# Memory gates moved to the seven-product jobs, branch sums added on VectorE, two squares of the residual put off

## Chip, core and metric

One Trainium2 chip, one of its NeuronCores. The metric is the time of one launch on the device, in microseconds; three runs of the kernel before gave a median of 1319.66 us (1317.09 to 1323.9). The core has five engines with queues of their own (TensorE = PE, VectorE = DVE, ScalarE = ACT, GpSimd = POOL, SyncE = SP) and 16 DMA engines that all queues share. SP computes nothing here; it issues nearly all transfers, in the order of its queue.

## The reference

One layer of a streaming encoder for 640 tokens (512 of a prompt, 8 x 16 of samples), width 1024, all in float32. The part that matters:

```python
xn = rmsnorm(x, norm_mix_g)
u, v, cq, ckv, kr, qm, ga, gb, gc = split(xn @ w_in)        # one combined projection
o_gm, o_mla, o_mem = gMLP(u, v), latent_attention(cq, ckv, kr), memory_attention(qm)
merged = (sigmoid(ga) * (o_gm @ w_br_gm)
          + sigmoid(gb) * (o_mla @ w_br_mla)
          + sigmoid(gc) * (o_mem @ w_br_mem))
h = x + merged @ w_out
y = h + (silu(hn @ ffn_w_gate) * (hn @ ffn_w_up)) @ ffn_w_down   # hn = rmsnorm(h, norm_ffn_g)
```

The sigmoid is made as (tanh(g/2) + 1), with the factor 1/2 in the weights.

## The kernel before

**Two ways to multiply.** Every float32 operand is split into a high and a low part, and one product is three matmuls (low weight x high data, high x high, high x low). `lin` does a block of 128 outputs plainly: 8 slices of the inner dimension, two halves of 320 tokens, three matmuls, so 48 matmuls of 128x320, with a weight of 128x1024 that ACT casts (L84) and DVE subtracts (L79). The later stage, `post`, uses a scheme of seven products for two by two blocks: a job makes 256 outputs by seven products of 12 matmuls, 84 matmuls where the plain way takes 96. Its weights come as four quarters of 128x512 (`wraws`, L1064), and sums of quarters are made on DVE (`wq`, L1048 and L1054). Sums of the data blocks (tiles `xc`) are made once and serve every job on the same data.

**Order of the stages.** Memory keys and attention; the memory branch (about 185 to 330 us), in which the latent attention's first projections and the samples' queries are interleaved; latent attention; then `post`: jobs in pairs, the two jobs' products alternating, for u and the gates of gMLP and latent attention; then the branch products of latent attention (`mla`, four jobs) and gMLP (`gm`, four jobs), each by eight direct products "a" to "h", 96 matmuls; then the output projection (`w_o`, four jobs), gate/up and down.

**The memory branch.** `branch` goes through 8 blocks of 128 outputs. A block is a gate (48 matmuls `psb<-xh` or `xl`) and a product with `w_br_mem` (48 matmuls `psb<-oh` or `ol`); `merge` scales the gate on DVE, takes the tanh on ACT, and multiplies on DVE into the accumulator `acc`, which is stored to `accspill` every two blocks. From block 3 on the samples' queries lie in between (`cqs`, `qns` and `tmp,perm` in the rows). Raw weights go through one pool of `WR` slots, three here.

**The branch sums.** A `mla` job loads its stored gate (tile `th`), multiplies it with the products (L1380) and stores the result to `tdram` (`t<-th`). In the first `gm` pair `acc_load` loads the four parts of `accspill` into `raw`, and four transfers on POOL's queue add the `t` parts to it in flight (L1447):

```python
raw_load(sa, [self.accd[j] for j in range(4)])()
for j in range(4):
    nc.gpsimd.dma_start(out=sa["t"][:, j], in_=tdram[j], accum_op=ALU.add)
```

The `gm` jobs then add their own products to `raw` (L1383), and from `raw` DVE and ACT make the data blocks of the output projection. Tiles `th` and the loads of h share a pool of five slots.

**The residual.** `out_job` adds a job's products to a part of x, stores it, squares it on ACT (L1478) and adds the square into `rbc` on DVE (L1483). `stats` makes the norm of it before the last product of the first gate/up job.

Of the kernel before, what the change touches and what calls it, by code (L numbers as in the profile page):

```python
# [18 lines left out]
T = 640  # L19
# [37 lines left out]
class Builder:  # L57
# [153 lines left out]
    def build(self):  # L211
        tc, nc, a = self.tc, self.nc, self.a
        ctx = ExitStack()
        pool = lambda name, side="left", **kw: tc.alloc_tile_pool(name=name, bufs=1, side=side, reuse_waits="tile", **kw)
        self.pool = pool
        self.WB, self.WR = 2, 3
        self.wx, self.wn = None, 0
        cp = pool("const")
        self.ap = pool("acc")
        self.tp = pool("tmps")  # L220
        self.wp = pool("wts", "right")
        self.pp = None
        self.psum(sc=6, tr=1, pv=1)

        self.ident = cp.tile([128, 128], F32, name="ident")
        self.ones = cp.tile([128, 128], F32, name="ones")
        self.gvec = cp.tile([128, 45], F32, name="gvec")
        self.mhalf = cp.tile([128, 8], F32, name="mhalf")
        self.rbc = cp.tile([128, T], F32, name="rbc")
        nc.gpsimd.memset(self.ones, 1.0)  # L230
        nc.gpsimd.memset(self.mhalf, -0.5)
        self.dma(self.gvec, a["gvec"])
        self.rtok = cp.tile([128, 8], F32, name="rtok")
        nc.scalar.activation(self.rtok, self.mhalf, AF.Exp)
# [12 lines left out]
        self.mem_branch(s2, ob)  # L247
        ob.release()
        x1.release()

        self.mla(s2)
        s2.release()
        self.post()
        self.tp.release()
        self.ap.release()
        cp.release()
        self.pp.release()
# [297 lines left out]
            out.append((h, l))  # L555
        return out

    def merge(self, m, pg, z, first):

        nc = self.nc  # L560
        th = self.tmp()
        self.scaled(th, pg)
        nc.scalar.activation(th, th, AF.Tanh, scale=0.5)
        if first:
            if m == 0:
                self.accT = self.ap.tile([128, 8, T], F32, tag="acc", bufs=1, name="acc")
            self.acc[m] = self.accT[:, m, :]
            nc.vector.scalar_tensor_tensor(self.halves(self.acc[m]), self.halves(th), 1.0, z, op0=ALU.add, op1=ALU.mult)
        else:
            nc.vector.scalar_tensor_tensor(self.halves(th), self.halves(th), 1.0, z, op0=ALU.add, op1=ALU.mult)  # L570
            nc.gpsimd.tensor_tensor(self.acc[m], self.acc[m], th, op=ALU.add)

    def gate(self, n, m):
        w = self.wload(self.a["w_g_" + n][m], 1024)
        pg = self.psb()
        self.lin(pg, w, self.xs)
        return pg

    def branch(self, n, os_, first=False, hooks={}, pg=None):
        a = self.a  # L580
        if first:
            self.acc = [None] * 8
        for m in range(8):
            if m or pg is None:
                pg = self.gate(n, m)
            for f in hooks.get(2 * m, ()):
                f()
            w = self.wload(a["w_br_" + n][m], 1024)
            po = self.psb()
            self.lin(po, w, os_)  # L590
            self.merge(m, pg, po[:, :, :HN], first)
            if m % 2:
                self.dma(self.accd[m // 2], self.accT[:, m - 1:m + 1, :])
            for f in hooks.get(2 * m + 1, ()):
                f()

# [57 lines left out]
    def mem_branch(self, s2, ob):  # L654

        a = self.a
        tp = self.pool("s2t")
        self.mla_consts(s2)
        st = {}

        def ckv():
            st["ckv"] = self.proj(tp, [0, 1])
            st["kr"] = self.proj(tp, [2])[0]

        def rckv():
            st["rkv"] = self.squared(st["ckv"])

        def nckv():
            self.ckvn, self.ckvs = self.normed(st["ckv"], st["rkv"], G_KV, "ckv")
            for k in range(2):  # L670
                self.dma(a["ckvT_o"][128 * k:128 * k + 128, :], st["ckv"][k])

        def cq():
            self.rope_key(st["kr"])
            st["cq"] = self.proj(tp, [3, 4, 5])

        def rcq():
            st["rq"] = self.squared(st["cq"])

        def ncq():  # L680
            self.cqn, self.cqs = self.normed(st["cq"], st["rq"], G_Q, "cq")

        ckv()
        os_ = self.split_o(self.omem, ob)
        hooks = HOOKS(rckv, nckv, cq, rcq, ncq)
        for pr in range(4):
            hooks[7 + 2 * pr] = [lambda pr=pr: self.sample_qn(s2, pr)]
            hooks[8 + 2 * pr] = [lambda pr=pr: self.sample_qr(pr)]
        self.branch("mem", os_, first=True, hooks=hooks)
        tp.release()  # L690
        self.t2.release()

# [516 lines left out]
    def post(self):  # L1209
# [69 lines left out]
        for tag, bufs in (("r21", 3), ("r22", 3), ("ws", 2), ("wl", HB), ("wh", HB), ("r12", 2), ("r11", 2)):  # L1279
            self.W.tile([128, 512], F32R if tag[0] == "w" and tag != "ws" else F32, tag=tag, bufs=bufs, name=tag)  # L1280

        gdram = {n: [self.tc.dram_tile([128, 2, T], F32, name="g" + n + str(j)) for j in range(4)] for n in ("mla", "gm")}

        def gate_job(n, j):
            cnt = []

            def done(g, q):
                cnt.append(q)
                if len(cnt) == 4:
                    nc.scalar.activation(g, g, AF.Tanh, scale=0.5)  # L1290
                    self.dma(gdram[n][j], g)
            return {"ap": a["w_g_" + n][j], "kp": 4, "xc": xc, "ev": self.ev_form(lambda: pair("g"), done)}

        def u_job(j):
            cnt = []
# [57 lines left out]
        jobs[0][1]["post"] = {2: [v_end(0)], 3: [v_end(1)]}  # L1353
        jobs += [[u_job(j), gate_job("gm", j)] for j in range(4)]
        jobs[1][0]["post"] = {2: [v_end(2)]}
        jobs += [[gate_job("mla", 2), gate_job("mla", 3)]]
        for x in jobs[2:]:
            x[1]["post"] = {5: [run_later], 2: [run_later]}
        pairs = [(x, self.LATER) for x in jobs]
# [5 lines left out]
        xb, make = self.operands(src, True)  # L1365


        tdram = [self.tc.dram_tile([128, 2, T], F32, name=f"t{j}") for j in range(4)]

        def branch_job(n, j, xb):  # L1370
            st = {}

            def load():
                st["th"] = pair("th")
                self.dma(st["th"], gdram[n][j])

            def ev(q, ps):
                ix = (slice(None), q[0], slice(HN * q[1], HN * q[1] + HN))
                t = st["th"][ix]
                nc.vector.scalar_tensor_tensor(t, t, 1.0, ps, op0=ALU.add, op1=ALU.mult)  # L1380
                if n == "gm":
                    acc = sa["t"][:, j][ix]
                    nc.vector.tensor_tensor(acc, acc, t, op=ALU.add)  # L1383
                elif q == (1, 0):
                    self.dma(tdram[j], st["th"])
            return {"ap": a["w_br_" + n][j], "kp": 4, "xc": xb, "ev": ev, "load": load}

        def raw_load(src, tiles):
            def f():
# [50 lines left out]
        add_d([branch_job("gm", j, xb) for j in range(4)])  # L1440
        sa = {}
        xo, mko = self.operands(sa)

        def acc_load():
            raw_load(sa, [self.accd[j] for j in range(4)])()
            for j in range(4):
                nc.gpsimd.dma_start(out=sa["t"][:, j], in_=tdram[j], accum_op=ALU.add)  # L1447
        hook(pairs[-2][0][0], "a", acc_load, "pre")
        B = pairs[-1][0][1]
        for at, f in (("a", lambda: (mko(1, 0, 2), mko(5, 0, 2))), ("b", lambda: (mko(6, 0, 2), mko(3, 0, 2))), ("c", lambda: mko(7, 0, 2)),  # L1450
                      ("d", lambda: (mko(1, 2, 4), mko(5, 2, 4))),
# [5 lines left out]
        sh = {}  # L1457
        xf, make = self.operands(sh)
        s = self.rbc

        def out_job(j):
            st = {}
# [8 lines left out]
            def done(q):  # L1471
# [3 lines left out]
                nc.scalar.activation(sh["t"][:, j, m, ns], h[:, m, ns], AF.Copy, scale=self.g(G_FFN + 2 * j + m))  # L1475
                if q == (1, 0):
                    self.dma(self.hdram[j], h)
                    nc.scalar.activation(h, h, AF.Square)  # L1478
                    if j == 0:
                        nc.vector.tensor_tensor(s, h[:, 0, :], h[:, 1, :], op=ALU.add)  # L1480
                    else:
                        for m in range(2):
                            nc.vector.tensor_tensor(s, s, h[:, m, :], op=ALU.add)  # L1483
            return {"ap": a["w_o"][j], "kp": 4, "xc": xo, "ev": lambda p, ps: st["ev"](p, ps), "load": load}

        out = [out_job(j) for j in range(4)]
# [33 lines left out]

        n0 = len(pairs)
        add([x for j in range(NF // 2) for x in gu_jobs(j)])
        hook(pairs[n0][0][0], 7, stats, "pre")

        ys = {}

# [136 lines left out]
def _prepare(i):  # L1663
# [20 lines left out]
    for p in range(128):  # L1684
# [13 lines left out]
        "w_qm": _pack(wqm),  # L1698
        "ck": mk.reshape(8, 256, 4, 2, 128).transpose(2, 0, 4, 3, 1),
        "cv": mv.reshape(8, 2, 128, 4, 256).transpose(3, 0, 2, 1, 4),  # L1700
        "w_g_gm": _packs(ga), "w_g_mla": _packs(gb), "w_g_mem": _pack(gc),
        "w_br_gm": _packs(i["w_br_gm"][0]), "w_br_mla": _packs(i["w_br_mla"][0]), "w_br_mem": _pack(i["w_br_mem"][0]),
        "w_kvq": _pack(np.concatenate([wckv, wkr, wkr, wcq], 1)),
        "w_uqn": uqn,
# [42 lines left out]
```

## Time and profile before

| | |
|---|---|
| median of three runs | 1319.66 us |
| profiled execution | 1319.9 us, of which span 1318.2 us |
| PE busy | 1272.3 us (97%), 8800 matmuls |
| DVE busy | 954.7 us (72%) |
| ACT busy | 640.5 us (49%) |
| POOL busy | 67.4 us (5%) |
| mean granted clock of TensorE | 0.995 of full speed |

The span runs from the first to the last instruction; 1.7 us of the execution lie around it. PE's matmuls are pipelined, so that the duration of one says little; the distance from start to start is what a matmul costs. A few per cent of the matmul records are missing from the trace.

### The profile page before, as it was taken

The numbers are of one execution on the slowest core, as the hardware profiler recorded it, in microseconds if no ns is written. First come the engines' busy times: TensorE is split into PE (matmuls) and PEld (weight loads), VectorE is DVE, ScalarE is ACT, GpSimd is POOL, SyncE is SP. The second block draws the span as 40 slices with busy tenths as digits, with TensorE's granted clock in tenths as the row PEclk, the third lists the DMA queues.
The fourth block names the chain that finished last, engine by engine and source line by source line (L and its number), as shares of the span: only waits on it lengthen the run. The fifth ranks groups of instructions, "written<-read, shape, count | busy, mean of one in ns | idle before, by whom it ended". The sixth has DMA issues, their size and how long they took to land.

```text
span 1318.2 us, 22764 instructions
## 1 busy us (share of the span) xinstructions
PE 1272.3 (97%) x8800; PEld 1226.9 (93%) x8800; DVE 954.7 (72%) x1723; ACT 640.5 (49%) x1263; POOL 67.4 (5%) x84
## 2 busy tenths in 40 slices
PE   7899999999999999999999999989999999998997
PEld 7898899999988889899999999989999999998997
DVE  7844354432578787688874457998889888899986
ACT  6734342222466656585554222665455455655444
POOL 5200001000000120000000000000000000000000
PEclk9999999999999999999999999999999999999999
DMA  7874622233532462243368862426344334342443
GB/s 228 261 265 160 211 95 90 76 113 120 171 90 80 160 234 81 73 144 133 134 227 294 258 197 88 133 80 195 119 135 137 103 101 136 101 164 86 145 133 122
DMA packets 83020, 193.56 MB, mean 147 GB/s; under 512 B 8480, under 2 KB 21920, under 8 KB 82912
## 3 DMA queue, kind: packets, MB, share of 16 engines
q1 hardware_dynamic: 80416, 182.93, 41.6%
q0 software_dynamic: 2224, 8.91, 2.5%
q8 instruction: 69, 1.13, 0.4%
q14 instruction: 39, 0.32, 0.1%
q10 hardware_dynamic: 272, 0.26, 0.1%
HBM read 159.41 MB, written 31.62 MB: 145 GB/s over the span
## 4 chain that ended last, share of the span: by engine, by line
PE 62%; DVE 18%; DMA 8%; issue 7%; ACT 4%; POOL 0%; SPq 0%; POOLq 0%; DVEq 0%; ACTq 0%
PE psb L65 18%; PE psX L1111 15%; PE psc L65 11%; PE psY L1111 6%; DVE wl L79 6%; PE psv L65 4%; PE psZ L1111 3%; DVE xc L79 2%; DVE ws L1054 2%; PE ppv L65 1%; DMA wr<-in_w_fd 1%; DMA wr<-in_w_fu 1%; ACT wh L84 1%; PE ptr L65 1%; DMA wr<-in_w_o 1%
## 5 line engine op out<-in xcount | busy, mean ns | idle before, releaser
L84 ACT CAST wh<-wr 128x512 fp32r<-128x512 f32 (+5 forms) x372 | 219.5, 610 | 216.7 <-PE psX L1111 62.4
L79 DVE TENSOR_TENSOR wl<-wr,wh 128x512 fp32r<-128x512 f32 (+5 forms) x372 | 253.1, 694 | 77.9 <-ACT wh L84 77.5
L1111 PE MATMUL psX<-xc,wh 128*128 128x320 f32 x1344 | 298.1, 310 | 0.0
L1111 PEld LDWEIGHTS psX<-xc,wh 128*128 128x128 f32 x1344 | 226.1, 189 | 0.0
L1111 PE MATMUL psX<-xc,wl 128*128 128x320 f32 x672 | 210.4, 313 | 12.3 <-DVE th L1380 4.9
L1111 PE MATMUL psY<-xc,wh 128*128 128x320 f32 x672 | 150.2, 310 | 0.0
L1111 PEld LDWEIGHTS psX<-xc,wl 128*128 128x128 f32 x672 | 126.8, 189 | 17.5 <-DVE th L1380 5.7
L84 ACT CAST wh<-ws 128x512 fp32r<-128x512 f32 x138 | 85.0, 619 | 77.2 <-DVE ws L1054 64.0
L1111 PEld LDWEIGHTS psY<-xc,wh 128*128 128x128 f32 x672 | 113.5, 189 | 0.0
L1111 PE MATMUL psY<-xc,wl 128*128 128x320 f32 x336 | 105.2, 313 | 7.6 <-DVE wl L79 5.7
L79 DVE TENSOR_TENSOR wl<-ws,wh 128x512 fp32r<-128x512 f32 x138 | 93.1, 685 | 17.9 <-ACT wh L84 17.2
L1111 PE MATMUL psZ<-xc,wh 128*128 128x320 f32 x400 | 89.2, 311 | 0.0
L65 PE MATMUL psb<-xh,wl 128*128 128x320 f32 x352 | 83.1, 317 | 0.0
L65 PE MATMUL psb<-xl,wh 128*128 128x320 f32 x352 | 80.9, 310 | 0.0
L65 PE MATMUL psb<-xh,wh 128*128 128x320 f32 x352 | 80.2, 309 | 0.0
L1111 PEld LDWEIGHTS psY<-xc,wl 128*128 128x128 f32 x336 | 63.6, 189 | 10.0 <-DVE wl L79 7.8
L1111 PEld LDWEIGHTS psZ<-xc,wh 128*128 128x128 f32 x400 | 67.3, 189 | 0.5 <-issue 0.5
L65 PEld LDWEIGHTS psb<-xh,wl 128*128 128x128 f32 x352 | 57.5, 188 | 5.9 <-issue 5.8
L1111 PE MATMUL psZ<-xc,wl 128*128 128x320 f32 x200 | 62.2, 311 | 0.0
L1054 DVE TENSOR_TENSOR ws<-ws,wr 128x512 f32<-128x512 f32 x92 | 61.5, 683 | 0.1
L84 ACT CAST xc<-raw 128x1280 fp32r<-128x1280 f32 (+1 forms) x36 | 37.3, 1054 | 47.8 <-DVE raw L1383 19.0
L65 PEld LDWEIGHTS psb<-xh,wh 128*128 128x128 f32 x352 | 58.8, 188 | 0.0
(406 smaller groups left out, 2927.6 us busy)
## 6 DMA issues: line engine op xcount, KB each, us to landing
wr<-in_w_fg SPq DMA_DIRECT2D x44, 256.0 KB, 3.4
wr<-in_w_fu SPq DMA_DIRECT2D x44, 256.0 KB, 3.7
cache<-in_ck SPq DMA_DIRECT2D x8, 1024.0 KB, 8.2
cache<-in_cv SPq DMA_DIRECT2D x8, 1024.0 KB, 7.4
wr<-in_w_fd SPq DMA_DIRECT2D x32, 256.0 KB, 3.7
aspill<-g SPq DMA_DIRECT2D x11, 640.0 KB, 3.1
raw<-aspill SPq DMA_DIRECT2D x11, 640.0 KB, 5.3
wr<-in_w_ft SPq DMA_DIRECT2D x32, 192.0 KB, 2.5
```

The costliest lines, as they stand in the source:

```text
L65: i = self.nc.tensor.matmul(out, lhsT=l, rhs=r, start=start, stop=stop)
L79: self.nc.vector.tensor_tensor(out, a, b, op=ALU.subtract)
L84: self.nc.scalar.copy(h, src)
L1054: nc.vector.tensor_tensor(src, x, z, op=ALU.add)
L1111: self.nc.tensor.matmul(ps, lhsT=lw[:, ws], rhs=rx[:, k, :], start=first and k == 0 and i == 0, stop=last and k == kp - 1 and i == 2, skip ...
```

## The change

- The memory gates leave `branch`. They become four seven-product jobs in two pairs behind the last pair of latent-attention gates. `branch` keeps only the products with `w_br_mem`; ACT copies them into a tile `z`, stored to `accspill`. A memory gate job loads its part of `z`, takes the tanh and forms (tanh + 1) x z with one DVE instruction of 128x1280; the result is stored to `gmem`.
- A `mla` job loads its part of `gmem` beside its gate, adds it to its own product on DVE (128x1280, L1373 after) and stores the sum over `accspill`. The `gm` pair loads `accspill` alone: the `tdram` tiles and the four adding transfers of POOL are gone.
- The squares of output jobs 2 and 3 are made after products 6 and 3 of the second job of the first gate/up pair, and `stats` after its product 7.
- The raw-weight pool has four slots, and `w_g_mem` is packed in quarters.

```diff
-        self.WB, self.WR = 2, 3
+        self.WB, self.WR = 2, 4
...
-    def branch(self, n, os_, first=False, hooks={}, pg=None):
+    def branch(self, os_, hooks):
+
         a = self.a
-        if first:
-            self.acc = [None] * 8
+        z = self.ap.tile([128, 8, T], F32, tag="acc", bufs=1, name="z")
         for m in range(8):
-            if m or pg is None:
-                pg = self.gate(n, m)
             for f in hooks.get(2 * m, ()):
                 f()
-            w = self.wload(a["w_br_" + n][m], 1024)
+            w = self.wload(a["w_br_mem"][m], 1024)
             po = self.psb()
             self.lin(po, w, os_)
-            self.merge(m, pg, po[:, :, :HN], first)
+            self.nc.scalar.copy(self.halves(z[:, m, :]), po[:, :, :HN])
             if m % 2:
-                self.dma(self.accd[m // 2], self.accT[:, m - 1:m + 1, :])
+                self.dma(self.accd[m // 2], z[:, m - 1:m + 1, :])
...
         def gate_job(n, j):
             cnt = []
+            st = {}
+
+            def load():
+                st["z"] = pair("z")
+                self.dma(st["z"], self.accd[j])
 
             def done(g, q):
                 cnt.append(q)
                 if len(cnt) == 4:
                     nc.scalar.activation(g, g, AF.Tanh, scale=0.5)
+                    if n == "mem":
+                        nc.vector.scalar_tensor_tensor(g, g, 1.0, st["z"], op0=ALU.add, op1=ALU.mult)
                     self.dma(gdram[n][j], g)
-            return {"ap": a["w_g_" + n][j], "kp": 4, "xc": xc, "ev": self.ev_form(lambda: pair("g"), done)}
+            return {"ap": a["w_g_" + n][j], "kp": 4, "xc": xc, "ev": self.ev_form(lambda: pair("g"), done),
+                    "pre": {6: [load]} if n == "mem" else {}}
...
-        jobs += [[gate_job("mla", 2), gate_job("mla", 3)]]
+        jobs += [[gate_job("mla", 2), gate_job("mla", 3)]] + [[gate_job("mem", j), gate_job("mem", j + 1)] for j in (0, 2)]
...
+            def more():
+                st["z"] = pair("z")
+                self.dma(st["z"], gdram["mem"][j])
...
                 elif q == (1, 0):
-                    self.dma(tdram[j], st["th"])
-            return {"ap": a["w_br_" + n][j], "kp": 4, "xc": xb, "ev": ev, "load": load}
+                    nc.vector.tensor_tensor(st["th"], st["th"], st["z"], op=ALU.add)
+                    self.dma(self.accd[j], st["th"])
+            return {"ap": a["w_br_" + n][j], "kp": 4, "xc": xb, "ev": ev, "load": load, "pre": {"d": [more]} if n == "mla" else {}}
...
-        def acc_load():
-            raw_load(sa, [self.accd[j] for j in range(4)])()
-            for j in range(4):
-                nc.gpsimd.dma_start(out=sa["t"][:, j], in_=tdram[j], accum_op=ALU.add)
-        hook(pairs[-2][0][0], "a", acc_load, "pre")
+        hook(pairs[-2][0][0], "a", raw_load(sa, [self.accd[j] for j in range(4)]), "pre")
...
                 if q == (1, 0):
                     self.dma(self.hdram[j], h)
-                    nc.scalar.activation(h, h, AF.Square)
-                    if j == 0:
-                        nc.vector.tensor_tensor(s, h[:, 0, :], h[:, 1, :], op=ALU.add)
+                    if j < 2:
+                        squares()
                     else:
-                        for m in range(2):
-                            nc.vector.tensor_tensor(s, s, h[:, m, :], op=ALU.add)
+                        late.append(squares)
...
-        hook(pairs[n0][0][0], 7, stats, "pre")
+        for p in (6, 3):
+            hook(pairs[n0][0][1], p, lambda: late.pop(0)())
+        hook(pairs[n0][0][1], 7, stats)
```

PE's queue in the memory branch, where the queries of one pair of heads for the samples begin, before (`cqs` and `qns` are the samples' latent and query, `xh` and `xl` the gate's data, `wr` a raw weight):

```order
L65 MATMUL psb<-cqs,wr 128x128 x6
L65 MATMUL psb<-xh,wl 128x320 x2
L65 MATMUL psb<-xh,wh 128x320 x2
L65 MATMUL psc<-qns,wr 128x128 x4
L65 MATMUL psb<-xl,wh 128x320 x2
L65 MATMUL psb<-xh,wl 128x320 x2
...
L65 MATMUL psb<-xl,wh 128x320 x2
L65 MATMUL psc<-cqs,wr 128x128 x3
L65 MATMUL psb<-oh,wl 128x320 x2
L65 MATMUL psb<-oh,wh 128x320
L65 MATMUL psc<-tmp,perm 128x128
```

and the same place after:

```order
L65 MATMUL psb<-cqs,wr 128x128 x6
L65 MATMUL psb<-oh,wl 128x320 x2
L65 MATMUL psb<-oh,wh 128x320 x2
L65 MATMUL psc<-qns,wr 128x128 x4
L65 MATMUL psc<-cqs,wr 128x128 x3
L65 MATMUL psb<-ol,wh 128x320 x2
L65 MATMUL psb<-oh,wl 128x320
L65 MATMUL psc<-tmp,perm 128x128
```

The 48 matmuls of the gate between the queries and the branch product are gone; the branch product (`oh`, `ol`) starts right behind the first six query matmuls.

SP's queue from the end of the `mla` jobs to the first weights of the output projection, before (`th` is a job's gate and product, `t` the stored product, `raw` the sum):

```order
L76 DMA raw<-accspill 128x1280 x3
L1064 DMA wr<-in_w_br_gm 128x512 x2
L76 DMA raw<-accspill 128x1280
L1064 DMA wr<-in_w_br_gm 128x512 x2
L76 DMA th<-ggm_6141 128x1280
L1064 DMA wr<-in_w_br_gm 128x512 x2
L76 DMA t_6149<-th 128x1280
L76 DMA t_6150<-th 128x1280
L1064 DMA wr<-in_w_br_gm 128x512
L1064 DMA wr<-in_w_o 128x512
L76 DMA th<-ggm_6142 128x1280
L76 DMA h<-in_xT 128x2x640
```

and after:

```order
L76 DMA raw<-accspill 128x1280 x2
L1041 DMA wr<-in_w_br_gm 128x512 x3
L76 DMA th<-ggm_5676 128x1280
L76 DMA accspill<-th 128x1280 x2
L76 DMA raw<-accspill 128x1280 x2
L1041 DMA wr<-in_w_br_gm 128x512
L1041 DMA wr<-in_w_o 128x512 x2
L76 DMA th<-ggm_5677 128x1280
L76 DMA th<-ggm_5678 128x1280
L1041 DMA wr<-in_w_o 128x512 x3
L76 DMA h<-in_xT 128x2x640
```

The second half of `raw` and both gates of the last `gm` pair now stand behind the stores of the last `mla` pair, and the second load of `w_o` stands ahead of the gates.

## Rows read from the trace of the kernel before

**Rows 1.** The page: the span, and PE's busy time, share and instructions.

```profile
span 1318.2 us, 22764 instructions
PE 1272.3 (97%) x8800; PEld 1226.9 (93%) x8800; DVE 954.7 (72%) x1723; ACT 640.5 (49%) x1263; POOL 67.4 (5%) x84
```

**Rows 2.** PE's waits: whom for, us in total, times, longest.

```profile
PE psc L65 <- DVE wl L79: 5.4, 5, 1.5
PE psX L1111 <- DVE th L1380: 4.9, 3, 3.9
```

**Rows 3.** Windows, memory branch and seven-product gates: busy by engine, clock, DMA share, GB/s.

```profile
231.00:264.00 33.00, 33.00 (x226) 32.52 (x225) 14.00 (x17) 8.23 (x12) 2.09 (x1) 1.00 0.24 79
627.00:660.00 33.00, 33.00 (x232) 33.00 (x231) 28.53 (x48) 17.00 (x31) 0.00 (x0) 1.00 0.41 142
```

**Rows 4.** Memory branch, one period: start, duration, engine, line, what, count, wait.

```profile
274.79 1.50 PE L65 MATMUL psb<-cqs,wr 128*128 128x128 f32 x12
...
276.33 0.38 SPq L76 DMA_DIRECT2D wr<-in_w_br_mem  x1
...
282.11 1.05 ACT L84 CAST wh<-wr 128x1024 fp32r<-128x1024 f32 x1 [3.79 <-DMA wr<-in_w_br_mem]
...
283.20 1.23 DVE L79 TENSOR_TENSOR wl<-wr,wh 128x1024 fp32r<-128x1024 f32 x1 [7.31 <-ACT wh L84]
...
284.79 0.54 PE L65 MATMUL psb<-oh,wl 128*128 128x320 f32 x2
...
292.31 1.39 PE L65 MATMUL psb<-cqs,wr 128*128 128x128 f32 x11
```

**Rows 5.** PE's timeline from the branch stage to gate/up.

```profile
700.14 0.41 PE L1111 MATMUL psY<-xc,wl 128*128 128x320 f32 x1 [1.92 <-ACT xc L84]
...
730.72 0.42 PE L1111 MATMUL psX<-xc,wl 128*128 128x320 f32 x1 [0.61 <-DVE th L1380]
...
733.12 0.42 PE L1111 MATMUL psX<-xc,wl 128*128 128x320 f32 x1 [0.37 <-DVE th L1380]
...
784.86 0.45 PE L1111 MATMUL psX<-xc,wh 128*128 128x320 f32 x2
...
787.50 0.45 PE L1111 MATMUL psX<-xc,wh 128*128 128x320 f32 x2
791.85 0.41 PE L1111 MATMUL psX<-xc,wl 128*128 128x320 f32 x1 [3.90 <-DVE th L1380]
...
881.76 0.56 PE L1111 MATMUL psX<-xc,wl 128*128 128x320 f32 x2 [0.52 <-ACT g L1132]
...
887.67 0.41 PE L1111 MATMUL psX<-xc,wl 128*128 128x320 f32 x1 [0.36 <-ACT u L1132]
```

**Rows 6.** Windows behind the longest wait: columns as in rows 3.

```profile
793.00:797.00 4.00, 4.00 (x19) 4.00 (x18) 2.03 (x4) 0.00 (x0) 0.00 (x0) 0.59 0.74 215
797.00:801.00 4.00, 4.00 (x30) 4.00 (x29) 2.03 (x5) 0.00 (x0) 0.00 (x0) 1.00 0.64 247
```

**Rows 7.** The chain that ended last, 755 to 800 us: start, duration, what.

```profile
770.13 8.28 DMA wr<-in_w_o
```

**Rows 8.** DVE's timeline: the wait ahead of PE's, and one instruction of 128x1280.

```profile
778.50 0.69 DVE L1054 TENSOR_TENSOR ws<-wr 128x512 f32<-128x512 f32 x1 [5.87 <-DMA wr<-in_w_o]
...
905.97 1.48 DVE L1500 TENSOR_TENSOR g<-g,rbc 128x1280 f32<-128x1280 f32 x1
```

**Rows 9.** DMA queues, 768 to 780 us: packets, MB, share of the 16 engines' time.

```profile
q0 software_dynamic: 276, 1.25, 51.4%
q1 hardware_dynamic: 581, 1.26, 28.5%
```

**Rows 10.** Transfers issued 720 to 800 us: count, size, median us to landing.

```profile
raw<-t POOLq DMA_DIRECT2D x4, 640.0 KB, 10.7
wr<-in_w_o SPq DMA_DIRECT2D x9, 256.0 KB, 3.9
```

**Rows 11.** ACT's timeline at the first gate/up pair.

```profile
885.52 1.27 ACT L1478 ACTIVATE h<-h 128x1280 f32<-128x1280 f32 x1
...
887.20 0.41 ACT L1132 COPY u<-psX 128x320 f32<-128x320 f32 x1
```

More of the change, by code (lines that the diff above doesn't have):

```diff
@@ L556, in split_o @@
         return out
[L558 to L563, printed above, removed]
-        if first:
[L565 to L577, printed above, removed]
-    def branch(self, n, os_, first=False, hooks={}, pg=None):
+    def branch(self, os_, hooks):
         a = self.a
-        if first:
-            self.acc = [None] * 8
+        z = self.ap.tile([128, 8, T], F32, tag="acc", bufs=1, name="z")
         for m in range(8):
-            if m or pg is None:
-                pg = self.gate(n, m)
             for f in hooks.get(2 * m, ()):
                 f()
-            w = self.wload(a["w_br_" + n][m], 1024)
+            w = self.wload(a["w_br_mem"][m], 1024)
             po = self.psb()
             self.lin(po, w, os_)
-            self.merge(m, pg, po[:, :, :HN], first)
+            self.nc.scalar.copy(self.halves(z[:, m, :]), po[:, :, :HN])
             if m % 2:
-                self.dma(self.accd[m // 2], self.accT[:, m - 1:m + 1, :])
+                self.dma(self.accd[m // 2], z[:, m - 1:m + 1, :])
             for f in hooks.get(2 * m + 1, ()):
@@ L688, in mem_branch @@
             hooks[8 + 2 * pr] = [lambda pr=pr: self.sample_qr(pr)]
-        self.branch("mem", os_, first=True, hooks=hooks)
+        self.branch(os_, hooks)
         tp.release()
@@ L1280, in post @@
             self.W.tile([128, 512], F32R if tag[0] == "w" and tag != "ws" else F32, tag=tag, bufs=bufs, name=tag)
-        gdram = {n: [self.tc.dram_tile([128, 2, T], F32, name="g" + n + str(j)) for j in range(4)] for n in ("mla", "gm")}
+        gdram = {n: [self.tc.dram_tile([128, 2, T], F32, name="g" + n + str(j)) for j in range(4)] for n in ("mla", "gm", "mem")}
         def gate_job(n, j):
             cnt = []
+            st = {}
+            def load():
+                st["z"] = pair("z")
+                self.dma(st["z"], self.accd[j])
             def done(g, q):
@@ L1365, in post @@
         xb, make = self.operands(src, True)
-        tdram = [self.tc.dram_tile([128, 2, T], F32, name=f"t{j}") for j in range(4)]
         def branch_job(n, j, xb):
@@ L1459, in post @@
         s = self.rbc
+        late = []
         def out_job(j):
@@ L1477, in done, with squares @@
                     self.dma(self.hdram[j], h)
-                    nc.scalar.activation(h, h, AF.Square)
-                    if j == 0:
-                        nc.vector.tensor_tensor(s, h[:, 0, :], h[:, 1, :], op=ALU.add)
-                    else:
-                        for m in range(2):
-                            nc.vector.tensor_tensor(s, s, h[:, m, :], op=ALU.add)
+                    if j < 2:
+                        squares()
+                    else:
+                        late.append(squares)
+            def squares():
+                h = st["h"]
+                nc.scalar.activation(h, h, AF.Square)
+                if j == 0:
+                    nc.vector.tensor_tensor(s, h[:, 0, :], h[:, 1, :], op=ALU.add)
+                else:
+                    for m in range(2):
+                        nc.vector.tensor_tensor(s, s, h[:, m, :], op=ALU.add)
             return {"ap": a["w_o"][j], "kp": 4, "xc": xo, "ev": lambda p, ps: st["ev"](p, ps), "load": load}
@@ L1700, in _prepare @@
         "cv": mv.reshape(8, 2, 128, 4, 256).transpose(3, 0, 2, 1, 4),
-        "w_g_gm": _packs(ga), "w_g_mla": _packs(gb), "w_g_mem": _pack(gc),
+        "w_g_gm": _packs(ga), "w_g_mla": _packs(gb), "w_g_mem": _packs(gc),
         "w_br_gm": _packs(i["w_br_gm"][0]), "w_br_mla": _packs(i["w_br_mla"][0]), "w_br_mem": _pack(i["w_br_mem"][0]),
```

## The prediction

> **What bounds the kernel now.** I read the page first: of a span of 1318.2 us PE is busy for 1272.3, with 8800 matmuls in the trace [rows 1]. The reader is to see two ways to a gain: fewer matmuls, or shorter waits of PE, which are 46 us in all. So I read next what a matmul costs, and then PE's waits one by one.
>
> A matmul's cost is the distance between starts. In a stretch without waits 18 matmuls of 320 columns lie between 784.86 and 787.50 us [rows 5]: 2.64 / 18 = 0.1467 us. The windows agree: 226 matmuls in 33.00 us in the memory branch, 232 in the seven-product gates, both at full clock and with PE busy throughout [rows 3] (0.146 and 0.142, with some smaller matmuls between). So both ways of multiplying run at the same pitch, and a matmul saved in either is worth 0.147 us as long as nothing else becomes late.
>
> Of PE's waits in the stages that the change touches, one stands out: the wait for `th` of 3.9 us, out of 4.9 in three times [rows 2]. It ends at 791.85 [rows 5]. Its price is more than its length: in 793 to 797 us the granted clock is 0.59 of full speed, close to the 1.2 GHz level, and 19 matmuls run where the next 4 us, at 2.4 GHz, have 30 [rows 6]. (30 - 19) x 4 / 30 = 1.47 us, so that the wait costs 5.4 us together. The chain that ended last leads back from there to a load of `w_o`, issued at 770.13 and 8.28 us under way [rows 7]. DVE, which runs in order, stood 5.87 us for it until 778.50 [rows 8], with the products' multiplications and the operands of the output projection queued behind; it caught up only when PE had run dry.
>
> **The change, part by part.**
>
> *Products.* Eight plain gates of 48 matmuls are 384; four seven-product jobs of 84 are 336. 48 x 0.1467 = **-7.0 us**. This is the firmest term. The Trainium skill, "TensorE: Matmul & The Clock Gate", section "Wait — 56ns, not 53.3ns?", gives N/2.4 GHz and about 2.5 ns as the gap of matmuls back to back, which is 135.8 ns for 320 columns; by that estimate the term would be -6.5. The row is 8% longer here, and decides.
>
> *What these jobs need beside PE.* In the stretch of seven-product gates DVE is busy for 28.53 of 33.00 us and PE does not wait [rows 3]. The memory gates need the same, with one DVE instruction of 128x1280 in each job, 1.48 us by the nearest row [rows 8]. Two of these in a pair of 168 matmuls (24.6 us) raise DVE from 0.86 to 0.98 of the time, if that stretch were typical; it is one with u jobs in part, so I cost it at nothing, hidden by PE's 24.6 us. If that cover is gone, the four cost 5.9 at most.
>
> *The transition to the branch jobs.* PE waits 1.92 us there for an `xc` of ACT already [rows 5]. The last two multiplications by z now stand among the subtractions that make these operands: nothing if DVE waits for ACT there, 2 x 1.48 = 3.0 if it does not. I take **+0.5**, near the first, since the wait's releaser is ACT.
>
> *The adding transfers.* Four loads into `raw` and four additions in flight become four plain loads; four loads of z are new. So the branch stage still moves twelve pieces of 640 KB: four stores, four loads, and four additions that become loads. In 768 to 780 us POOL's queue took 51.4% of the engines' time for 1.25 MB, SP's 28.5% for 1.26 MB [rows 9]: a byte added in flight occupied the engines 1.8 times as long as a byte loaded. An addition took 10.7 us to land in the median [rows 10], and the late load of `w_o` ran beside the last of them, where the median of nine such loads is 3.9 us [rows 10]. With 3.9 the load issued at 770.13 lands at 774.0, 4.4 us sooner, and the 3.90 us of PE and the slow 1.47 us behind them go: -5.4. If the load is as late as before, 0. I take **-4.4**, near the first: the margin over 3.9 is only 0.5 us, and a part of the wait may stay without a drop of the clock.
>
> The Trainium skill speaks against this term: "DMA: Bandwidth & Descriptors", section "Rules for kernel authors", says that to spread transfers over SP, ACT and GpSimd does not help, since all run on the same 16 engines and interleave. By it a change of queue with the same bytes leaves the load at 8.28 us and the term is 0. The queues' shares [rows 9] say that these bytes were not equal in cost, so I follow the row and keep the rule as a rival.
>
> *The sums on DVE.* Four additions of 1.48 us, two in each `mla` pair, whose 192 matmuls take 28.2 us. The first pair ends with two small waits of PE for `th`, 0.61 and 0.37 [rows 5]. The additions stand beside just these multiplications, so the waits can go (-1.0, when the DMA engines have more room) or each grow by an addition that comes first (+1.5). I take **0**.
>
> *Squares put off.* At the first gate/up pair PE waits 0.52 and 0.36 us for copies by ACT [rows 5]; the second copy, at 887.20, stands right behind a square of 1.27 us [rows 11]. Put off, the squares are out of its way: **-0.8**, bounds -0.9 and +1 (the squares as late as before, behind other copies). The later norm has work of whole products between it and its first user.
>
> *The memory branch without gates.* Here the change takes a cover away. A period with the samples' queries is 292.31 - 274.79 = 17.5 us; without 48 matmuls it is 10.5. One weight of `w_br_mem` per period is issued at 276.33, its cast starts at 282.11 (5.8 us), and cast and subtraction end at 284.43, 8.1 us after the issue and 0.36 us ahead of the first matmul of 284.79 that needs it [rows 4]. After the change SP issues it when the queries' raw weights are free, which I put at 3.5 us after the period's start: 0.75 us for six query matmuls (half of the twelve that take 1.50 [rows 4]), 4 x 0.147 for the branch's, about 1 us for the seven smaller ones, and 1.2 us for the release and three issues of 0.38 [rows 4]. It is needed behind the next period's six query matmuls, at 10.5 + 0.75 = 11.3; it is ready at 3.5 + 8.1 = 11.6. So each of four periods waits 0.3 us; with the load as quick as 3.9 [rows 10], nothing; with 8.28 [rows 7], 2.8 us and a slow clock. I take **+1.0**, bounds 0 and (2.8 + 1.47) x 4 = +17. The fourth raw slot can also ease waits at the start, of which PE has 5.4 us for DVE's weights [rows 2]; they are waits for DVE, not for a load, so 0, at best -1.
>
> Sum: -7.0 + 0.5 - 4.4 - 0.8 + 1.0 = -10.7. The profiled execution took 1319.9 us, 1.7 around its span and 0.2 above the median of 1319.66, which I neglect: **1309 us**. With all terms at their good ends (-7.0 - 5.4 - 1.0 - 0.9) it is 1305.6, and with half of the load's term gone 1311.4.
>
> **Rivals.**
> A. *The load of `w_o` stays late.* For it: the bytes are the same, in the same stretch. Against it: the queues' shares [rows 9]. 1319.9 - 7.0 - 0.8 + 1.5 = 1313.6. The rule of the Trainium skill's page on DMA, above, would make this the outcome.
> B. *SP's queue becomes the wait.* The second half of `raw` may be loaded only when the last sums of `mla` are stored, and SP, in order, holds back the last weight of `gm`, two of `w_o` and the two gates until a store has landed. A landing is 3.9 to 8.28 us by the loads' rows [rows 7, 10]. Against it: that load was issued at 770.13, and its raw slot came free only then, so some of the delay lies where nothing is due. If the wait at 791.85 doubles: 1313.6 + 3.9 = 1317.5.
> C. *Slower: the memory branch waits for its weights.* If a load there takes 9 us and not 5.8, a period waits 0.3 + 3.2 = 3.5 us, and drops the clock for 1.5 more: 5.0 x 4 = 20 in place of 1: 1328. It decides, against all the gains, from a landing of about 8.7 us, just above the longest load of my rows [rows 7]. For it: the margin before was 0.36 us [rows 4]. Against it: the engines' share in that stretch is 0.24 [rows 3], and the gates' weights no longer load there.
>
> **How the numbers follow.** Forecast 0.66, A 0.18, B 0.09, C 0.07. Half a per cent (6.6 us) is about what a measurement of this kernel can tell from no change; faster by more is below 1313.3. Of the forecast nearly all (0.64) lies there, of A 0.07, of B nothing: 0.71. Same is the rest of A and of the forecast and nearly all of B: 0.21. Slower is C with a rest: 0.08. The range goes from 1304, just under all good ends with the start's 1 us (1304.6), to 1317, which takes in A and half of B; the forecast's own is 1304 to 1313.
>
> **What would show it.** 48 matmuls fewer, and no wait in the two pairs of memory gates. No wait of several us for `th` at the pair of `gm` jobs, and a load of `w_o` that lands in some 4 us; if it lands in 8 with POOL's queue empty, A is right. In the memory branch windows of PE fully busy, periods of 10.5 us and no drop of the clock; a PE that waits for `wl` or `wh` there is C. In SP's queue no issue of `w_o` that moves behind the stores by more than 4 us; if it does, B. I am wrong in kind if the time is above 1313, and in size if the first term holds but the second is less than half.

## The result, and the profile after

The changed kernel takes 1306.36 us in the median (four runs, 1304.65 to 1307.41) against 1321.78 us for the kernel before beside it: a ratio of 0.9885, 95% interval 0.9849 to 0.992. The forecast was 1309 us, faster, in a range of 1304 to 1317. The profiled execution has a span of 1305.7 us, 12.5 below the one before.

The page of the changed kernel, to be held against [rows 1]:

```profile
span 1305.7 us, 22778 instructions
PE 1263.4 (97%) x8752; PEld 1218.2 (93%) x8752; DVE 979.0 (75%) x1763; ACT 657.8 (50%) x1303; POOL 66.1 (5%) x80
```

48 matmul records fewer, and 8.9 us less of PE; the other 3.6 us of the span were waits. DVE has 24 us more to do. The two pairs of memory gates lie between 643 and 692 us of the changed kernel; PE does not wait there, and DVE is busy for 33.36 of 49 us (columns as in [rows 3]):

```profile
643.00:692.00 49.00, 49.00 (x337) 49.00 (x336) 33.36 (x53) 26.53 (x49) 0.00 (x0) 1.00 0.67 230
```

PE's timeline in the changed kernel, at the places of [rows 5]: the transition to the branch jobs, the wait for `th`, and ACT's copy at the first gate/up pair.

```profile
694.64 0.41 PE L1088 MATMUL psY<-xc,wl 128*128 128x320 f32 x1 [1.92 <-ACT xc L84]
783.12 0.41 PE L1088 MATMUL psX<-xc,wl 128*128 128x320 f32 x1 [1.42 <-DVE th L1368]
870.79 0.56 PE L1088 MATMUL psX<-xc,wl 128*128 128x320 f32 x2 [0.52 <-ACT g L1109]
```

The transition waits as long as before; the wait for `th` is 1.42 us instead of 3.90; the two small ones of the first `mla` pair have no row any more (the second profile of this kernel, changed_again, has one of 0.44), nor has the copy of u, while that of g still ends a wait of 0.52. The windows behind the wait for `th`, columns as in [rows 6]:

```profile
783.00:787.00 4.00, 3.88 (x26) 3.88 (x27) 3.29 (x7) 0.00 (x0) 0.00 (x0) 1.00 0.65 173
787.00:791.00 4.00, 4.00 (x30) 4.00 (x29) 1.43 (x3) 0.00 (x0) 0.00 (x0) 1.00 0.92 343
```

The granted clock stays at its upper level, 2.4 GHz, where it fell to 0.59 before. So between these two profiles this wait gave 2.5 us and the slow clock behind it 1.5.

The memory branch in the changed kernel, one weight of `w_br_mem` from its issue to its use (timeline, all engines; a `cqs` row of 12 records is six instructions of the order):

```profile
266.51 1.50 PE L65 MATMUL psb<-cqs,wr 128*128 128x128 f32 x12
...
270.38 0.33 SPq L76 DMA_DIRECT2D wr<-in_w_br_mem  x1
...
275.64 1.05 ACT L84 CAST wh<-wr 128x1024 fp32r<-128x1024 f32 x1 [4.99 <-DMA wr<-in_w_br_mem]
...
276.73 1.23 DVE L79 TENSOR_TENSOR wl<-wr,wh 128x1024 fp32r<-128x1024 f32 x1 [4.17 <-ACT wh L84]
...
277.06 1.50 PE L65 MATMUL psb<-cqs,wr 128*128 128x128 f32 x12
...
278.32 0.54 PE L65 MATMUL psb<-oh,wl 128*128 128x320 f32 x2
```

The period is 277.06 - 266.51 = 10.55 us, as forecast, and the weight is issued 3.87 us into it, for the next one. Its low part is ready at 277.96 (276.73 + 1.23), 0.36 us before PE takes it. No period waits for `w_br_mem` here; the one wait of this branch, 1.08 us, has another cause (see five_slots).

### The profile page after: what moved, and what is told of

The parts are those of the page before. It is cut to its first block, busy times and chain, and to the rows that moved or that the text cites. A ratio compares the mean times of both kernels' runs of the same rounds, so it can differ in the third digit from the quotient of the medians.

```text
span 1305.7 us, 22778 instructions
## 1 busy us (share of the span) xinstructions
PE 1263.4 (97%) x8752; PEld 1218.2 (93%) x8752; DVE 979.0 (75%) x1763; ACT 657.8 (50%) x1303; POOL 66.1 (5%) x80
## 4 chain that ended last, share of the span: by engine, by line
PE 63%; DVE 19%; DMA 7%; issue 6%; ACT 3%; POOL 0%; SPq 0%; POOLq 0%; DVEq 0%; ACTq 0%
PE psX L1088 19%; PE psb L65 14%; PE psc L65 11%; PE psY L1088 8%; DVE wl L79 6%; PE psZ L1088 5%; PE psv L65 3%; DVE ws L1031 2%; DVE xc L79 2%; PE ppv L65 1%; DMA wr<-in_w_fd 1%; ACT wh L84 1%; DMA wr<-in_w_o 1%; DMA wr<-in_w_g_gm 1%; PE ptr L71 1%
## 5 line engine op out<-in xcount | busy, mean ns | idle before, releaser
L84 ACT CAST wh<-ws 128x512 fp32r<-128x512 f32 x150 | 92.5, 620 | 84.6 <-DVE ws L1031 74.2
L79 DVE TENSOR_TENSOR wl<-ws,wh 128x512 fp32r<-128x512 f32 x150 | 101.2, 685 | 20.7 <-ACT wh L84 19.9
L1031 DVE TENSOR_TENSOR ws<-ws,wr 128x512 f32<-128x512 f32 x100 | 66.9, 683 | 0.2
L84 ACT CAST xc<-raw 128x1280 fp32r<-128x1280 f32 (+1 forms) x36 | 37.4, 1054 | 38.0 <-DVE raw L1371 18.1
L1031 DVE TENSOR_TENSOR ws<-wr 128x512 f32<-128x512 f32 x50 | 34.3, 687 | 27.1 <-DMA wr<-in_w_fu 11.6
L65 PE MATMUL psb<-xh,wl 128*128 128x320 f32 x224 | 53.5, 320 | 0.0
L190 ACT ACTIVATE P<-psc,nb 128x256 f32<-128x256 f32 (+4 forms) x60 | 30.2, 505 | 43.8 <-DVE nb L184 38.4
L65 PE MATMUL psb<-xl,wh 128*128 128x320 f32 x224 | 51.6, 311 | 0.0
L155 POOL TENSOR_TENSOR rstd<-ms,mhalf 128x5 f32<-128x5 f32 (+2 forms) x7 | 9.3, 1329 | 834.7 <-DVE ms L153 834.7
```

Source lines behind the costliest of these rows:

```text
L65: i = self.nc.tensor.matmul(out, lhsT=l, rhs=r, start=start, stop=stop)
L79: self.nc.vector.tensor_tensor(out, a, b, op=ALU.subtract)
L84: self.nc.scalar.copy(h, src)
L155: nc.gpsimd.tensor_tensor(r[:rows, :n], v[:rows, :n], self.mhalf[:rows, :n], op=ALU.pow)
L190: nc.scalar.activation(P, ps, AF.Exp, bias=nb, scale=scale, accum_out=se)
L1031: nc.vector.tensor_tensor(src, x, z, op=ALU.add)
```

## Experiments

Ratios are to the kernel before, run on the same chip in the same session; 0.001 is 1.3 us.

| run | contents | median us | ratio, 95% interval |
|---|---|---|---|
| gates_alone | gates | 1339.76 | 1.0130 (1.0107 to 1.0153) |
| sums_alone | sums | 1315.41 | 0.9951 (0.9935 to 0.9967) |
| slots_alone | slot | 1319.49 | 0.9979 (0.9967 to 0.9990) |
| squares_alone | squares | 1319.12 | 0.9978 (0.9968 to 0.9988) |
| gates_and_slots | gates, slot | 1313.84 | 0.9948 (0.9928 to 0.9968) |
| adds_on_pool | all but the sums | 1314.18 | 0.9944 (0.9928 to 0.9959) |
| squares_early | all but the squares | 1308.97 | 0.9891 (0.9875 to 0.9907) |
| no_slots | all but the slot | 1332.28 | 1.0078 (1.0056 to 1.0099) |
| changed_again | all | 1306.46 | 0.9892 (0.9872 to 0.9911) |
| loads_on_pool | all, sums loaded by POOL | 1304.41 | 0.9873 (0.9852 to 0.9893) |
| late_half | all, half the sums loaded later | 1305.15 | 0.9883 (0.9863 to 0.9902) |
| five_slots | all, five slots | 1305.05 | 0.9876 (0.9857 to 0.9896) |

**gates_alone.** The diff's `branch`, `gate_job` and packing on the kernel before; then

```diff
-            raw_load(sa, [self.accd[j] for j in range(4)])()
+            raw_load(sa, [gdram["mem"][j] for j in range(4)])()
```

with POOL adding the `t` parts onto the stored memory gates.

> The memory gates as seven-product jobs and nothing else of the change: the branch sums are still added in flight by four transfers of POOL (onto the stored memory gates instead of the old sum), three raw-weight slots, squares where they were. Theory (the two traces read together): 48 matmuls fewer, -7.0 us, less 1.1 us for a wait in the memory branch and 1.4 us lost around the two new pairs of gates: -4.5 us, with the long wait for th before the output projection still there. Rival (the products are worth their full price and the losses belong to the other edits): -7 us. Rival (three raw slots do not cover the memory branch's weights any more): windows in the memory branch with PE below 0.95 busy, and -3 us or less.

Slower by 1.3%, which neither the theory nor the first rival had; the second rival had the place and not the size. The windows of this kernel (columns as in [rows 3]):

```profile
245.00:260.00 15.00, 9.77 (x56) 9.20 (x55) 2.25 (x5) 3.12 (x6) 0.45 (x1) 0.77 0.41 135
260.00:275.00 15.00, 11.46 (x81) 10.89 (x81) 2.25 (x5) 3.12 (x6) 0.46 (x1) 1.00 0.28 93
275.00:290.00 15.00, 10.41 (x65) 9.84 (x64) 2.25 (x5) 3.12 (x6) 0.46 (x1) 0.89 0.39 137
290.00:305.00 15.00, 11.46 (x76) 10.89 (x76) 3.21 (x6) 3.96 (x7) 0.46 (x1) 0.94 0.34 110
```

PE is busy for 43 of 60 us, with the DMA engines' share at 0.41 or less: no engine is full. One weight on its way, in the timeline of this kernel:

```profile
245.22 1.50 PE L65 MATMUL psb<-cqs,wr 128*128 128x128 f32 x12
...
246.75 0.33 SPq L76 DMA_DIRECT2D wr<-in_w_br_mem  x1
...
251.91 1.04 ACT L84 CAST wh<-wr 128x1024 fp32r<-128x1024 f32 x1 [2.54 <-DMA wr<-in_w_br_mem]
252.98 1.22 DVE L79 TENSOR_TENSOR wl<-wr,wh 128x1024 fp32r<-128x1024 f32 x1 [1.72 <-ACT wh L84]
...
254.26 0.63 PE L65 MATMUL psb<-oh,wl 128*128 128x320 f32 x1 [4.36 <-DVE wl L79]
```

The weight is issued as the six query matmuls end, and is wanted 3 us later, in the same period. Before the change the same issue had the gate's 48 matmuls ahead of its use [rows 4]. The load itself is no slower than before: the cast starts 5.2 us after the issue, against 5.8 in [rows 4]. Four such waits make 13.4 us; the rest of the loss is smaller waits (2.0 for `qns`, 1.5 for `tmp`) and the clock.

**no_slots and slots_alone.** The edit and its reverse:

```diff
-        self.WB, self.WR = 2, 4
+        self.WB, self.WR = 2, 3
```

> The changed kernel with three raw-weight slots instead of four, everything else of the change kept. Theory (with the gates gone, the memory branch's weights need the fourth slot; the gates-alone run lost 20 us there): the same four waits of 2.7 to 4.4 us for the weight's low part, a clock below 1 in that stretch, 1326 to 1330 us, +20 to +23. Rival (the loss of the gates-alone run came from the adding transfers or from the late squares, not from the slots): within 3 us of the changed kernel.

> Only the fourth raw-weight slot. Theory (the first 60 us of the two traces differ by 1.5 us, where a load stands earlier in SP's queue): -1.5 us, with PE at the start of the second wave of weight waits (near 38 us) without its 0.8 us wait. Rival (the start differs by chance from launch to launch, or the prediction's own 0): within 0.5 us, with the same waits as before.

Without its fourth slot the changed kernel is 1.9% slower (1.0078 against 0.9892 and 0.9885), 25 us, a little above the theory's 20 to 23, with waits of 3.94, 2.67, 4.10 and 2.66 us for the same low part. That the other edits caused the loss of gates_alone is refuted. Alone, the slot is worth 0.2%, 2.8 us, more than its theory had. It isn't shown to be the start: the first 60 us end, by the last `psc<-wl,mh` with a wait, at 57.73 us with four slots alone, and at 58.84, 58.37, 57.14 and 57.17 in four profiles with three (the kernel before, sums_alone, squares_alone, gates_alone); and the wait near 38 us that the theory named is gone with four slots, but in the last two of these as well. Where it gains is open.

**gates_and_slots.** The two edits together.

> The memory gates as seven-product jobs and the fourth raw-weight slot, without the other edits (the sums added in flight by POOL, the squares where they were). Theory (the slot carries the memory branch without gates, and each is worth little without the other): no wait for a weight's low part between 240 and 300 us, periods of 10.5 us, -5 us on the kernel before within 2, 1315 to 1319 us, and the wait for th of 4 to 6 us still there. Rival (the loss in the gates-alone run has another part than the slots): +3 us or more.

As the theory had it: 0.9948, no wait for `wl` there. Against slots_alone the gates are worth 0.9948 / 0.9979 = 0.9969, or 4.1 us; the two intervals leave some 1 to 7 us, so that the 7.0 us of 48 matmuls are not excluded. In the profile the wait for `th` grew by 1.9 us. Waits for u and g are 0.6 us longer than in slots_alone (0.47 and 0.63 where that has 0.49); they lie at 529 and 532 us, in pairs ahead of the memory gates. Over all profiles these waits sum to 1.1 to 2.8 us with the gates moved and to 0.4 to 1.8 without, so that the 0.6 is likely and not sure. PE's timeline in this kernel:

```profile
692.78 0.41 PE L1088 MATMUL psY<-xc,wl 128*128 128x320 f32 x1 [1.92 <-ACT xc L84]
723.11 0.42 PE L1088 MATMUL psX<-xc,wl 128*128 128x320 f32 x1 [1.54 <-DVE th L1365]
785.50 0.64 PE L1088 MATMUL psX<-xc,wl 128*128 128x320 f32 x1 [5.79 <-DVE th L1365]
```

**sums_alone and adds_on_pool.** On the kernel before, `more` with the old sum; on the changed kernel the reverse, from `gdram["mem"]`:

```diff
+            def more():
+                st["z"] = pair("z")
+                self.dma(st["z"], self.accd[j])
...
-                    self.dma(tdram[j], st["th"])
+                    nc.vector.tensor_tensor(st["th"], st["th"], st["z"], op=ALU.add)
+                    self.dma(self.accd[j], st["th"])
...
```

> The branch sums alone: gates as before; an mla job loads its part of the stored sum, adds it on DVE and stores the result, and the gm pair loads it plainly, so that POOL adds nothing in flight. Theory (additions in flight hold the DMA engines longer per byte, so that the load of the output projection's weight lands late): the wait for th of 3.9 us falls below 2 us, no drop of the clock behind it, -4 to -5.5 us. Rival (the same bytes in the same stretch, so the load lands as late): the wait stays at 3 to 4 us and the time within 1 us of before.

> The changed kernel with the branch sums added in flight by POOL again (the plain loads bring the stored memory gates, four transfers add the products). Theory (additions in flight make the load of the output projection's weight late): the wait for th of 4 to 5 us is back, with the drop of the clock behind it, +4 to +6.5 us on the changed kernel, 1311 to 1313 us. Rival (the sums and the gates share one gain, and the order of SP's queue sets the wait): within 2 us of the changed kernel.

Both ways the sign and the place are the theory's: -6.5 us alone (0.0049 of 1322.5; the interval is 4.4 to 8.6), and 0.0052 to 0.0059, about 7.3 us, as the last edit (some 4 to 10 by the intervals). The wait for `th` is 1.21 us in sums_alone, with the clock at 1.00 behind it, and 6.18 in adds_on_pool, where the window behind it has half the clock:

```profile
786.73 0.64 PE L1088 MATMUL psX<-xc,wl 128*128 128x320 f32 x1 [6.18 <-DVE th L1365]
```

```profile
786.00:790.00 4.00, 3.27 (x12) 3.27 (x13) 3.90 (x8) 0.00 (x0) 0.00 (x0) 0.50 0.50 135
790.00:794.00 4.00, 4.00 (x29) 4.00 (x28) 0.22 (x1) 0.00 (x0) 0.00 (x0) 1.00 0.96 343
```

Against the changed kernel that is 4.3 to 4.8 us of waiting and, by an estimate, 1.6 of slow clock (12 matmuls in 3.27 busy us, where the next window's pitch makes 24): most of the 7.3. In sums_alone the profiles show 4.2 of the 6.5 (2.7 of waiting, 1.5 of clock); the rest is open.

PE's wait follows DVE's wait for the second load of `w_o`. Its first user on DVE, the sum `ws`, in sums_alone, adds_on_pool and the changed kernel, to be held against the 5.87 us of [rows 8]:

```profile
777.00 0.69 DVE L1054 TENSOR_TENSOR ws<-wr 128x512 f32<-128x512 f32 x1 [2.81 <-DMA wr<-in_w_o]
773.37 0.69 DVE L1031 TENSOR_TENSOR ws<-wr 128x512 f32<-128x512 f32 x1 [8.13 <-DMA wr<-in_w_o]
770.47 0.69 DVE L1031 TENSOR_TENSOR ws<-wr 128x512 f32<-128x512 f32 x1 [2.33 <-DMA wr<-in_w_o]
```

The shorter wait has two parts. The load lands sooner: 7.05 us after its issue in sums_alone and 6.6 in the changed kernel, where it takes 8.28 before and 10.54 in adds_on_pool. And DVE comes to it later, 4.3 us after the issue without the additions and 2.5 with them: in its program `ws` then stands behind an addition to `raw`, a subtraction of a weight and a multiplication that otherwise follow it. Of the 3.1 us between before and sums_alone, 1.2 are the landing and 1.8 this order. No run has the one without the other.

**loads_on_pool.** The queue without the addition:

```diff
-        hook(pairs[-2][0][0], "a", raw_load(sa, [self.accd[j] for j in range(4)]), "pre")
+        def acc_load():
...
+            for j in range(4):
+                nc.gpsimd.dma_start(out=sa["t"][:, j], in_=self.accd[j])
+        hook(pairs[-2][0][0], "a", acc_load, "pre")
```

> The changed kernel with the four loads of the stored sums issued by POOL instead of SP, plain loads without any addition. It tells what of the old cost was the queue and what the addition. Theory A (the addition itself is dear: POOL's queue took 1.8 times as long per byte): the share of POOL's queue per MB falls to that of SP's, and the time stays within 1 us of the changed kernel, or falls by 1 to 2 us since SP does not wait for the stores any more. Theory B (whatever POOL's queue moves is dear): the share per MB stays 1.8 times that of SP's, the wait for th grows to 3 us or more, +2 to +5 us.

The queues of adds_on_pool in 715 to 790 us, columns as in [rows 9]:

```profile
q1 hardware_dynamic: 5167, 14.75, 56.2%
q0 software_dynamic: 576, 2.62, 18.1%
```

and of loads_on_pool in the same stretch:

```profile
q1 hardware_dynamic: 5598, 15.42, 59.1%
q0 software_dynamic: 576, 2.62, 8.6%
```

The same 576 packets and 2.62 MB on POOL's queue: 6.9% of the engines' time per MB with the addition, 3.3% without, where SP's queue takes 3.8%. So the dear bytes were those of the addition, not of POOL's queue, and theory A holds. The time, 0.9873, is not told apart from the changed kernel's; the wait for `th` in the profile is 0.73 us.

**late_half.** The loads of parts 2 and 3 hooked to product "f" and no longer to "a":

```diff
-        hook(pairs[-2][0][0], "a", raw_load(sa, [self.accd[j] for j in range(4)]), "pre")
+        def acc_load(h):
...
+            for j in (2 * h, 2 * h + 1):
+                nc.sync.dma_start(out=sa["t"][:, j], in_=self.accd[j])
+        hook(pairs[-2][0][0], "a", lambda: acc_load(0), "pre")
+        hook(pairs[-2][0][0], "f", lambda: acc_load(1), "pre")
```

> The changed kernel with the second half of the stored sums loaded later: SP issues these two loads behind two loads of the output projection's weight and the two last gates, and no longer ahead of them, so that SP does not stand for the stores to land. Theory (what is left of the wait for th, 1.4 us, is SP's queue standing for the stores): the two loads of the weight are issued some 4 us sooner against the branch jobs, the wait for th falls below 0.8 us, -0.7 to -2 us on the changed kernel. Rival (the DMA engines are full there, and any order has the same bytes before the third load of the weight): the wait stays at 1 to 2 us, and the time within 0.5 us.

> The changed kernel as it is, for comparison on the same chip with the two others. Both theories: 1304 to 1308 us, a wait for th of 1 to 2 us.

The wait is 1.18 us here and 1.86 in changed_again, the ratios 0.9883 and 0.9892. The wait is the rival's; the 1.2 us between the ratios would be the theory's, but their intervals overlap, so the two are not told apart. SP's queue in changed_again stands for the stores of `th`, as rival B of the prediction had it:

```profile
752.17 2.35 SPq L76 DMA_DIRECT2D accspill<-th  x2
758.82 1.84 SPq L76 DMA_DIRECT2D raw<-accspill  x2
760.76 0.38 SPq L1041 DMA_DIRECT2D wr<-in_w_br_gm  x1
761.19 0.95 SPq L1041 DMA_DIRECT2D wr<-in_w_o  x2
762.19 1.71 SPq L76 DMA_DIRECT2D th<-ggm  x2
```

but moving the loads out of the way buys nothing clear. Against the branch jobs (DVE's first `th<-th,psY`) only the first load of `w_o` is issued sooner, by 6 us; the second, for which DVE waits first, is issued at the same place as in changed_again. That what is left is full DMA engines is the rival's account and not shown.

**squares_alone and squares_early.** The last two pieces of the diff, alone and undone.

> Only the two squares put off and the norm after product 7. Theory (the prediction's term): -0.8 us, the waits for the copies of g and u (0.52 and 0.36 us) gone. Rival (only the second copy stands behind a square): the wait for u gone, the one for g still there, -0.4 us. Rival (held tiles make the next jobs wait): +0.5 us or more.

> The changed kernel with the four squares and the norm where they were before. Theory (the squares alone gave -0.2%, of which the trace shows 0.36 us as a wait for the copy of u, and about 1 us in the jobs behind): +0.8 to +2.5 us, with the wait of 0.36 us for u back. Rival (the run of the squares alone differs by chance): within 0.5 us, and no wait back.

Alone 0.9978, with the wait for the copy of u gone and that for g still there; undone, 0.9891 where the changed kernel has 0.9885 and 0.9892, with a wait for u of 0.54 us back. The wait is shown; a gain in time is measured only from the kernel before, and 2.9 us is more than the 0.36 us seen there. slots_alone, which edits nothing here, gains as much (2.8), with the waits for `th`, g and u as long as before (3.90, 0.52 and 0.36). That a part of these gains, and of the 6.5 us of sums_alone, has nothing to do with what the edits touch is not excluded; no run tests it.

**five_slots.** `WR` = 5 in the changed kernel.

> The changed kernel with five raw-weight slots instead of four. Theory (four carry the memory branch with no time to spare: the third period's low part was ready about when PE wanted it, and a wait of 0 to 1.6 us for the samples' rotary query came and went between runs): the weights of the memory branch are issued sooner, the margin grows by a period's worth, and that wait is gone; at most -1.5 us. Rival (four are enough, and the wait has another cause, the cast of the next stage's weight ahead of the copy on ACT): the time within 1 us and the wait still there in some runs.

The subtraction of the weight at the place shown above starts at 274.33 us, not 276.73:

```profile
274.33 1.23 DVE L79 TENSOR_TENSOR wl<-wr,wh 128x1024 fp32r<-128x1024 f32 x1 [1.94 <-ACT wh L84]
```

so the margin grew by some 2 us, and this profile has no wait in the memory branch; nor has changed_again with four, while the first profile of the changed kernel has one of 1.08 us and late_half one of 1.57:

```profile
281.26 0.83 ACT L84 CAST wh<-wr 128x768 fp32r<-128x768 f32 x1 [1.05 <-DMA wr<-in_w_uqn]
282.58 0.49 PE L65 MATMUL psc<-tmp,perm 128*128 128x128 f32 x2 [1.08 <-ACT tmp L724]
```

The wait is where the rival put it: ACT's copy `tmp` stands behind the cast of another weight, `w_uqn`, for which ACT itself waits 1.05 us (1.55 in late_half). The slot helps as the theory had it: that weight is issued 0.9 us after the period's start with four slots (277.98) and 6.7 us before it with five (270.22). The time, 0.9876, is not told from the changed kernel's. No version here beats it clearly.

## Why the prediction was right, by its own steps

- **Products, -7.0.** Right in matmuls (48 records) and in what they free; 4.1 us of time by the medians (some 1 to 7) when the gates come with the slot, since longer waits for `th` (1.9) and probably for u and g (0.6) eat part of it.
- **Memory gate jobs hidden, and the transition.** The four DVE instructions are hidden: no wait in the two pairs (0.34 us in changed_again), and DVE is busy for 0.68 of that time, not for the 0.98 that I reckoned with. The transition's +0.5 was not there (1.92 us before and after).
- **The adding transfers, -4.4.** The cause was right: a byte added in flight is dear, and DVE's wait for a load of `w_o` passes on to PE. By the medians -6.5 to -7.3 us, beyond the good end of -5.4, though the intervals take that in. I sized the term by the wait of the kernel before; with the gates moved that wait would have been 5.8 to 6.2 us. The step in between was wrong: the load was to land in 3.9 us and took 6.6, and the one behind it 9.39, with POOL's queue empty. By the sign that I set (a load that lands in 8 us) that is rival A, but A's time did not come: what counts is how long DVE stands for the load, 2.33 and 0.60 us instead of 5.87, and about half of that came from an order of DVE's program that I had not looked at. That the term held is therefore in part luck; PE still waits 1.42 us. The rule of the Trainium skill, "DMA: Bandwidth & Descriptors", "Rules for kernel authors", that queues of different engines share the same DMA engines, agrees with loads_on_pool (3.3% of the engines' time per MB against 3.8%); it does not speak of what an addition costs in flight, which is where this term came from.
- **Squares, -0.8.** The copy of u was freed (0.36 us), the one of g not (0.52): it stood behind the product, not behind a square. Nor did the copy of u stand right behind the square, as I read [rows 11]: a cast of 0.60 us lies between.
- **The memory branch, +1.0.** The period of 10.5 us and the issue at 3.5 us were right (10.55 and 3.87). The use was placed 0.5 us too early, because I read twelve records as twelve instructions: they are six, and all 1.26 us of them stand ahead of the use. So no period waits for its weight. One step did fail in what it said of the slot: "The fourth raw slot can also ease waits at the start ... 0, at best -1". The slot decides whether a weight is issued for the next period or for its own, and is worth 25 us here. The estimate of 3.5 us silently held it; rival C, with its 20 us, has about the size of what the kernel loses without it, but not the reason: not slow loads, but an issue in the same period as the use.

Together, on the scale of the ratios: slot -2.8, gates -4.1, sums -7.3, squares -0.3, which is -14.5; the changed kernel measures -14.3 to -15.2. The first three are measured one on top of the other, so that their sum proves little, and each is known to within 1.5 to 3 us only. The forecast of -10.7 was short by about 4. By the medians the products gave 2.9 less than stated and the sums 2.9 more; the slot, put at 0, gave 2.8, and the 1.0 and 0.5 of loss did not come. That 1306 lies in the range rests on two errors that cancel, and on a slot that the change contained and the prediction had priced at nothing: without it the kernel takes 1332 us.

## What to carry to other kernels

When work is taken out of a loop, list what was loaded behind it: here 7 us of matmuls covered a weight's 8 us, and the gain of 4 us was to be had only with one more buffer, which alone is worth little. Price such a buffer together with the cut, and try the cut without it. An addition made by a transfer is not free because it costs no engine an instruction: count the DMA engines' time per byte, and who loads beside it. And look at where the engine that waits for a load stands in its own program: about half of the shorter wait here came from that.

## What the runs showed of the hardware

An addition in flight on POOL's queue took 1.8 times the engines' time per MB of SP's queue (adds_on_pool, 18.1% for 2.62 MB against 56.2% for 14.75 MB), a plain load on the same queue 0.9 times (loads_on_pool). The length of a wait alone did not tell whether the clock would fall behind it: the wait of 1.92 us that ends at 694.64 in the changed kernel has 0.72 in the window of 694 to 700 us, where one of 2.67 us that ends at 270.83 in gates_alone has 1.00 in that of 268 to 278. What decides is not shown here.
